# A softmax over 512 columns: stores held back, longer tiles towards the middle, and a first load in two halves

## The chip, the cores and the metric

The kernel runs on one core of a Trainium2 chip. The metric is the device time of one execution in microseconds (us); for the kernel before it is the median of eight runs. A profiled execution also gives a trace: what each engine and each DMA queue did, with times from the span's start.

## What is computed

A softmax along the last axis at temperature 2, on 16 x 1024 rows of 512 float32 numbers:

```python
batch, seq, dim = 16, 1024, 512
x_scaled = x / 2.0
x_max = np.max(x_scaled, axis=-1, keepdims=True)
exp_x = np.exp(x_scaled - x_max)
return exp_x / np.sum(exp_x, axis=-1, keepdims=True)
```

Every input byte is read once and every output byte is written once: 33.55 MB each way.

## The kernel before

The 16,384 rows are spread over the 128 partitions of the on-chip memory, so each partition has 128 rows of 512 floats to do. In what follows a "row" means one such row on every partition, 128 x 512 x 4 = 262,144 bytes. A tile is a group of consecutive rows that is loaded with one DMA and stored with one DMA. `PLAN` (line 11) lists the tiles: for each, how its rows are cut into chunks, and the place at which it stands in an arena of 100 rows (`ARENA`, 204,800 bytes per partition). The first tile has 3 rows, the second 7, then come seven of 15 and others of 7, 3 and 3; the work inside a tile goes by chunks of at most 5 rows.

All 128 rows don't fit in the arena at once. Tiles 0 to 7 (100 rows) have places of their own; tiles 8 to 11 take over the places of earlier ones, and can be loaded only after the stores of those have landed. The dictionary `behind` holds which.

Each chunk goes through three engines, and everything is done in place in the arena:

- VectorE takes the negated maximum of each row (line 85, one instruction for a chunk). It waits for the tile's load.
- ScalarE (ACT) does exp(0.5 x - 0.5 max) and the row sums (line 111, one instruction for a row). It waits for the chunk's maxima, counted by the semaphore `s_max`, and counts its chunks in `s_exp`.
- VectorE takes the reciprocals of the sums (line 94) and multiplies each row by its own (line 98). `s_mul` counts the chunks that are finished.

VectorE's order is written out: the maxima of chunk k, then the multiplies of chunk k - 2 (`LAG`). So while ScalarE works on one chunk, VectorE works on the one ahead and the one behind.

There are two DMA queues. The queue of ScalarE gets the loads of tiles 0 to 7 at the start, two of them ahead of the barrier with which the program begins. The queue of SP (SyncE) gets, in this order, the store of each tile as soon as its last chunk is multiplied (line 134), and, in between, the loads of tiles 8 to 11 (line 139), each after waits for the stores whose place it takes. Loads from the queue of ScalarE and stores from the queue of SP are carried out by the same 16 DMA engines. At the end SP waits for every store (line 141), and the program closes with a barrier of all engines, in which POOL (GpSimd) gathers the others.

Of the kernel before, what the change touches and what calls it, by code (L numbers as in the profile page):

```python
# [1 line left out]

# [4 lines left out]

PLAN = [
    ([3], 0), ([4, 3], 3), ([5] * 3, 10), ([5] * 3, 25), ([5] * 3, 40), ([5] * 3, 55),
    ([5] * 3, 70), ([5] * 3, 85), ([5] * 3, 10), ([4, 3], 3), ([3], 0), ([3], 25),
]
ARENA = 100
LAG = 2


@with_exitstack
def kernel(  # L20
    ctx: ExitStack,
    tc: tile.TileContext,
    x: bass.AP,
    out: bass.AP,
):
    nc = tc.nc
    fp32 = mybir.dt.float32

    xf = x.flatten_outer_dims()
    of = out.flatten_outer_dims()  # L30
    N, D = xf.shape
    P = nc.NUM_PARTITIONS
    n_rows = N // P
    assert sum(sum(c) for c, _ in PLAN) == n_rows

    arena = nc.alloc_sbuf_tensor("arena", (P, ARENA, D), fp32)
    negmax = nc.alloc_sbuf_tensor("negmax", (P, n_rows), fp32)
    sums = nc.alloc_sbuf_tensor("sums", (P, n_rows), fp32)
    recip = nc.alloc_sbuf_tensor("recip", (P, n_rows), fp32)

    tiles, chunks, base = [], [], 0
    for t, (cs, at) in enumerate(PLAN):
        r = sum(cs)
        tiles.append((base, r, at))
        o = 0
        for c in cs:
            chunks.append((t, base + o, c, at + o))
            o += c  # L50
        base += r
    last_chunk = {c[0]: k for k, c in enumerate(chunks)}

    def dram(ap, t):
        b, r, _ = tiles[t]
        return ap[b * P : (b + r) * P].rearrange("(p r) d -> p r d", r=r)

    def sb(t):
        _, r, at = tiles[t]
        return arena[:, at : at + r, :]  # L60


    behind = {}
    for t, (_, r, at) in enumerate(tiles):
        for u in range(t):
            _, ru, au = tiles[u]
            if at < au + ru and au < at + r:
                behind.setdefault(t, []).append(u)

    ld = [tc.alloc_semaphore(f"ld{t}") for t in range(len(tiles))]  # L70
    st = [tc.alloc_semaphore(f"st{t}") for t in range(len(tiles))]
    s_max = tc.alloc_semaphore("s_max")
    s_exp = tc.alloc_semaphore("s_exp")
    s_rec = tc.alloc_semaphore("s_rec")
    s_mul = tc.alloc_semaphore("s_mul")

    def issue_loads(begin, end):

        for t in range(begin, end):
            if t not in behind:  # L80
                nc.scalar.dma_start(out=sb(t), in_=dram(xf, t)).then_inc(ld[t], 16)

    def do_max(k):
        t, b, c, a = chunks[k]
        nc.vector.reduce_max(  # L85
            out=negmax[:, b : b + c],
            in_=arena[:, a : a + c],
            axis=mybir.AxisListType.X,
            negate=True,
        )._wait_ge(ld[t], 16).then_inc(s_max, 1)  # L90

    def do_mul(k):
        t, b, c, a = chunks[k]
        nc.vector.reciprocal(  # L94
            out=recip[:, b : b + c], in_=sums[:, b : b + c]
        )._wait_ge(s_exp, k + 1).then_inc(s_rec, 1)
        for r in range(c):
            ins = nc.vector.tensor_scalar_mul(  # L98
                out=arena[:, a + r],
                in0=arena[:, a + r],  # L100
                scalar1=recip[:, b + r : b + r + 1],
            )
            if r == 0:
                ins._wait_ge(s_rec, k + 1)
        ins.then_inc(s_mul, 1)

    def compute_and_store():

        for k, (t, b, c, a) in enumerate(chunks):
            for r in range(c):  # L110
                ins = nc.scalar.activation(  # L111
                    out=arena[:, a + r],
                    in_=arena[:, a + r],
                    func=mybir.ActivationFunctionType.Exp,
                    bias=negmax[:, b + r : b + r + 1],
                    scale=0.5,
                    accum_out=sums[:, b + r : b + r + 1],
                )
                if r == 0:
                    ins._wait_ge(s_max, k + 1)  # L120
            ins.then_inc(s_exp, 1)


        for k in range(len(chunks) + LAG):
            if k < len(chunks):
                do_max(k)
            if k >= LAG:
                do_mul(k - LAG)


        late = sorted(behind)
        for t in range(len(tiles)):
            nc.sync.wait_ge(s_mul, last_chunk[t] + 1)
            nc.sync.dma_start(out=dram(of, t), in_=sb(t)).then_inc(st[t], 16)
            while late and max(behind[late[0]]) <= t - 2:
                u = late.pop(0)
                for v in behind[u]:
                    nc.sync.wait_ge(st[v], 16)
                nc.sync.dma_start(out=sb(u), in_=dram(xf, u)).then_inc(ld[u], 16)
        for t in range(len(tiles)):  # L140
            nc.sync.wait_ge(st[t], 16)

    hook = nc.inst_callbacks[-1]
    nc.remove_inst_callback(hook)
    symbolic = nc._always_lower_symbolic_ap
    nc._always_lower_symbolic_ap = False
    here = str(nc.cur_bb)
    entry = nc.main_func.blocks[0]  # L150
    head, jumps = entry.instructions[:-5], entry.instructions[-5:]
    entry.instructions = []
    nc.switch_bb("main", None)
    issue_loads(0, 2)
    first = list(entry.instructions)
    at = next(k for k, i in enumerate(head) if type(i).__name__ == "InstDrain")
    entry.instructions = head[:at] + first + head[at:]
    issue_loads(2, len(tiles))
    compute_and_store()
    entry.instructions = list(entry.instructions) + jumps  # L160
    nc.switch_bb(here, None)
    nc._always_lower_symbolic_ap = symbolic
    nc.push_inst_callback(hook)


# [1 line left out]
_INS = ['x']  # L167
_OUTS = [((16, 1024, 512), 'float32')]


# [23 lines left out]
```

## Time and profile before

| What | us |
|---|---|
| Median of eight runs | 162.8 |
| Lowest and highest of the eight | 162.33, 163.19 |
| The profiled execution | 163.17 |
| Its span, first to last instruction | 161.4 |
| VectorE busy | 126.3 |
| ScalarE busy | 94.5 |
| VectorE idle until a load landed | 17.2 |
| ScalarE idle until a chunk's maxima were there | 43.5 |
| First store issued | 14.2 |
| Last store issued | 144.5 |

The sequence of VectorE, with the mean duration of each kind, comes from the groups of instructions with shapes kept apart: a maximum over five rows takes 2814 ns on its own and 2.73 us in sequence, over four 2283 ns, over three 1748 ns; a multiply of one row 482 ns (five in 2.07 us), a reciprocal about 175 ns. An exponential takes 710 ns.

How to read it: the DMA row of the page shows, for 40 equal slices of the span, the mean busy share of the 16 DMA engines in tenths, and the row under it what they moved in GB/s. Busy times of engines are shares of a whole in which any of them, or the DMA engines, may be what the others wait for. Time at the end, after the last instruction of the compute engines, is time in which only DMAs are under way.

### The profile page before, as it was taken

To read this page: it belongs to the slowest core of one execution; us is meant where nothing else is said; L and a number is where in the kernel's file an instruction comes from. 1 tells how busy PE (TensorE), PEld (TensorE's weight loads), DVE (VectorE), ACT (ScalarE), POOL (GpSimd) and SP (SyncE) were. 2 spreads that over 40 slices of the span, in tenths; PEclk is the share of its full clock that TensorE was granted. 3 is DMA by queue.
4 is the path that set the end of the run, shared out by engine and by line. 5 is a ranking of instruction groups with operands and counts; after the bars stand their busy time and mean duration, and the time that the engine had idled before them with its cause. 6 is when DMAs were issued, how large, how long until landed. Compare 5 with 4: busy or idle time off the path is not lost.

```text
span 161.4 us, 513 instructions
## 1 busy us (share of the span) xinstructions
DVE 126.3 (78%) x184; ACT 94.5 (59%) x257; POOL 0.2 (0%) x4
## 2 busy tenths in 40 slices
DVE  0485599999999999998499928999999999970000
ACT  0739087866688666796276651797666875630000
POOL 0000000000000000000000000000000000000000
DMA  7989999899999999999999999999999899999992
GB/s 284 465 388 472 404 439 437 344 447 418 464 381 451 411 457 404 449 434 426 442 411 457 396 459 411 449 402 460 390 434 477 381 472 404 457 434 419 399 418 96
DMA packets 3459, 67.13 MB, mean 416 GB/s; under 512 B 384, under 2 KB 384, under 8 KB 1152
## 3 DMA queue, kind: packets, MB, share of 16 engines
q1 hardware_dynamic: 2304, 40.90, 59.1%
q10 hardware_dynamic: 1152, 26.21, 38.6%
q14 instruction: 3, 0.02, 0.0%
HBM read 33.55 MB, written 33.55 MB: 416 GB/s over the span
## 4 chain that ended last, share of the span: by engine, by line
DVE 74%; DMA 10%; another core or an unknown queue 4%; issue 0%; DVEq 0%
DVE negmax L85 40%; DVE arena L98 32%; DMA arena<-in_x_dram 10%; DVE recip L94 2%; DVEq L189 0%
## 5 line engine op out<-in xcount | busy, mean ns | idle before, releaser
L111 ACT ACTIVATE arena<-arena,negmax 128x512 f32<-128x512 f32 x128 | 90.7, 710 | 43.5 <-DVE negmax L85 43.5
L85 DVE TENSOR_REDUCE negmax<-arena 128x5 f32<-128x2560 f32 (+2 forms) x28 | 72.3, 2586 | 17.2 <-DMA arena<-in_x_dram 17.2
L98 DVE TENSOR_SCALAR arena<-arena,recip 128x512 f32<-128x512 f32 x128 | 53.2, 482 | 1.0
L111 ACT ACTIVATION_READ_ACCUMULATOR arena<-arena,negmax 128x1 f32 x128 | 23.9, 187 | 0.0
L94 DVE RECIPROCAL recip<-sums 128x5 f32<-128x5 f32 (+2 forms) x28 | 4.9, 176 | 0.0
L111 ACT ACT_TABLE_LOAD x1 | 1.3, 1283 | 4.5 <-issue 4.5
L178 POOL MEMSET const-bfloat16-1.0<- 128x1 bf16 x1 | 0.1, 102 | 0.0
L178 POOL MEMSET const-uint8-127<- 128x1 uint8 x1 | 0.1, 102 | 0.0
L178 POOL MEMSET const-float32-0.0<- 128x1 f32 x1 | 0.1, 99 | 0.2 <-issue 0.2
L178 POOL MEMSET const-float32-1.0<- 128x1 f32 x1 | 0.1, 99 | 0.0
## 6 DMA issues: line engine op xcount, KB each, us to landing
out_dram<-arena SPq DMA_DIRECT2D x7, 3840.0 KB, 26.5
arena<-in_x_dram ACTq DMA_DIRECT2D x6, 3840.0 KB, 48.7
arena<-in_x_dram SPq DMA_DIRECT2D x1, 3840.0 KB, 35.9
out_dram<-arena SPq DMA_DIRECT2D x2, 1792.0 KB, 16.2
out_dram<-arena SPq DMA_DIRECT2D x3, 768.0 KB, 15.4
arena<-in_x_dram ACTq DMA_DIRECT2D x1, 1792.0 KB, 8.3
arena<-in_x_dram SPq DMA_DIRECT2D x1, 1792.0 KB, 39.6
arena<-in_x_dram SPq DMA_DIRECT2D x2, 768.0 KB, 38.8
```

What stands on the lines that cost most here:

```text
L85: nc.vector.reduce_max(out=negmax[:, b : b + c], in_=arena[:, a : a + c], axis=mybir.AxisListType.X, negate=True,)._wait_ge(ld[t], 16).the ...
L94: nc.vector.reciprocal(out=recip[:, b : b + c], in_=sums[:, b : b + c])._wait_ge(s_exp, k + 1).then_inc(s_rec, 1)
L98: ins = nc.vector.tensor_scalar_mul(out=arena[:, a + r], in0=arena[:, a + r], scalar1=recip[:, b + r : b + r + 1],)
L111: ins = nc.scalar.activation(out=arena[:, a + r], in_=arena[:, a + r], func=mybir.ActivationFunctionType.Exp, bias=negmax[:, b + r : b + r ...
L178: nc = _bacc.Bacc("TRN2", target_bir_lowering=False, num_devices=1)
```

## The change

The tiles are cut anew: ten instead of twelve, of 3, 5, 9, 15, 21, 21, 21, 15, 11 and 7 rows, and those of 21 rows are worked in chunks of seven. The first seven tiles (95 rows) have places of their own, and tiles 7, 8 and 9 take over places of earlier ones.

- The first tile's load is issued as two DMAs, partitions 0 to 63 from ScalarE's queue and partitions 64 to 127 from SP's (`FIRST`); both stand ahead of the opening barrier, and so does the load of tile 1.
- No store is issued before chunk 4 is multiplied (`HOLD`). The stores of tiles 0, 1 and 2 are issued at that point, one after the other.
- The late loads (tiles 7, 8, 9) move from SP's queue to ScalarE's. Each is issued from ScalarE after the exponentials of the tile that `AFTER` names (tile 4 for tile 7, tile 5 for tiles 8 and 9), after waits on ScalarE for the stores whose place it takes: stores 0, 1 and 2 for tile 7; 2 and 3 for tile 8; 3 for tile 9. SP now has only stores, beside the half of the first load.
- Stores that nobody's load waits for share one semaphore (`s_end`), and the waits at the end are POOL's.

The kernel's arithmetic and VectorE's order, the maxima of chunk k before the multiplies of chunk k - 2, stay.

```diff
--- before.py
+++ after.py
@@ -9,11 +9,19 @@
 
 
 PLAN = [
-    ([3], 0), ([4, 3], 3), ([5] * 3, 10), ([5] * 3, 25), ([5] * 3, 40), ([5] * 3, 55),
-    ([5] * 3, 70), ([5] * 3, 85), ([5] * 3, 10), ([4, 3], 3), ([3], 0), ([3], 25),
+    ([3], 0), ([5], 3), ([5, 4], 8), ([5] * 3, 17), ([7] * 3, 33), ([7] * 3, 54),
+    ([7] * 3, 75), ([5] * 3, 0), ([6, 5], 15), ([4, 3], 26),
 ]
 ARENA = 100
 LAG = 2
+
+HOLD = 4
+
+AFTER = {7: 4, 8: 5, 9: 5}
+
+EARLY = 2
+
+FIRST = [("scalar", [(0, 64)]), ("sync", [(64, 128)])]
 
 
 @with_exitstack
@@ -62,23 +70,34 @@
 
     behind = {}
     for t, (_, r, at) in enumerate(tiles):
+        assert at + r <= ARENA
         for u in range(t):
             _, ru, au = tiles[u]
             if at < au + ru and au < at + r:
                 behind.setdefault(t, []).append(u)
+    awaited = sorted({u for us in behind.values() for u in us})
 
     ld = [tc.alloc_semaphore(f"ld{t}") for t in range(len(tiles))]
-    st = [tc.alloc_semaphore(f"st{t}") for t in range(len(tiles))]
+    st = {t: tc.alloc_semaphore(f"st{t}") for t in awaited}
+    s_end = tc.alloc_semaphore("s_end")
     s_max = tc.alloc_semaphore("s_max")
     s_exp = tc.alloc_semaphore("s_exp")
     s_rec = tc.alloc_semaphore("s_rec")
     s_mul = tc.alloc_semaphore("s_mul")
 
-    def issue_loads(begin, end):
-
-        for t in range(begin, end):
-            if t not in behind:
-                nc.scalar.dma_start(out=sb(t), in_=dram(xf, t)).then_inc(ld[t], 16)
+    def do_load(engine, t, groups=((0, P),)):
+        for u in behind.get(t, []):
+            engine.wait_ge(st[u], 16)
+        for p, q in groups:
+            engine.dma_start(out=sb(t)[p:q], in_=dram(xf, t)[p:q]).then_inc(ld[t], 16)
+
+    def do_early():
+        for name, groups in FIRST:
+            do_load(getattr(nc, name), 0, groups)
+        for t in range(1, EARLY):
+            do_load(nc.scalar, t)
+
+    first_incs = 16 * sum(len(groups) for _, groups in FIRST)
 
     def do_max(k):
         t, b, c, a = chunks[k]
@@ -87,7 +106,7 @@
             in_=arena[:, a : a + c],
             axis=mybir.AxisListType.X,
             negate=True,
-        )._wait_ge(ld[t], 16).then_inc(s_max, 1)
+        )._wait_ge(ld[t], 16 if t else first_incs).then_inc(s_max, 1)
 
     def do_mul(k):
         t, b, c, a = chunks[k]
@@ -104,9 +123,16 @@
                 ins._wait_ge(s_rec, k + 1)
         ins.then_inc(s_mul, 1)
 
-    def compute_and_store():
-
+    def do_rest():
+
+
+        for t in range(EARLY, len(tiles)):
+            if t not in behind:
+                do_load(nc.scalar, t)
+        late = sorted(behind)
         for k, (t, b, c, a) in enumerate(chunks):
+            while late and last_chunk[AFTER[late[0]]] < k:
+                do_load(nc.scalar, late.pop(0))
             for r in range(c):
                 ins = nc.scalar.activation(
                     out=arena[:, a + r],
@@ -128,17 +154,19 @@
                 do_mul(k - LAG)
 
 
-        late = sorted(behind)
+        ends = 0
         for t in range(len(tiles)):
-            nc.sync.wait_ge(s_mul, last_chunk[t] + 1)
-            nc.sync.dma_start(out=dram(of, t), in_=sb(t)).then_inc(st[t], 16)
-            while late and max(behind[late[0]]) <= t - 2:
-                u = late.pop(0)
-                for v in behind[u]:
-                    nc.sync.wait_ge(st[v], 16)
-                nc.sync.dma_start(out=sb(u), in_=dram(xf, u)).then_inc(ld[u], 16)
-        for t in range(len(tiles)):
-            nc.sync.wait_ge(st[t], 16)
+            nc.sync.wait_ge(s_mul, max(last_chunk[t], HOLD) + 1)
+            ins = nc.sync.dma_start(out=dram(of, t), in_=sb(t))
+            if t in awaited:
+                ins.then_inc(st[t], 16)
+            else:
+                ins.then_inc(s_end, 16)
+                ends += 16
+
+        for t in awaited:
+            nc.gpsimd.wait_ge(st[t], 16)
+        nc.gpsimd.wait_ge(s_end, ends)
 
 
 
@@ -151,12 +179,11 @@
     head, jumps = entry.instructions[:-5], entry.instructions[-5:]
     entry.instructions = []
     nc.switch_bb("main", None)
-    issue_loads(0, 2)
+    do_early()
     first = list(entry.instructions)
     at = next(k for k, i in enumerate(head) if type(i).__name__ == "InstDrain")
     entry.instructions = head[:at] + first + head[at:]
-    issue_loads(2, len(tiles))
-    compute_and_store()
+    do_rest()
     entry.instructions = list(entry.instructions) + jumps
     nc.switch_bb(here, None)
     nc._always_lower_symbolic_ap = symbolic
```

## The prediction

> **What bounds the kernel now.** I read the page first: span, busy shares, the DMA rows. 163.17 us is the profiled execution's time, 161.4 its span, so 1.8 us lie outside; the median of the eight runs is 162.8.
>
> ```profile
> span 161.4 us, 513 instructions
> DVE 126.3 (78%) x184; ACT 94.5 (59%) x257; POOL 0.2 (0%) x4
> ...
> DMA  7989999899999999999999999999999899999992
> ...
> DMA packets 3459, 67.13 MB, mean 416 GB/s; under 512 B 384, under 2 KB 384, under 8 KB 1152
> ...
> q1 hardware_dynamic: 2304, 40.90, 59.1%
> q10 hardware_dynamic: 1152, 26.21, 38.6%
> ```
>
> No engine is full, and the DMA row is full from the second slice to the second last. Queue q10 is ACT's (the 100 resident rows of 262,144 B are 26.21 MB), q1 is SP's. Their packets took 59.1 + 38.6 = 97.7% of 161.4 us, so 157.7 us of each DMA engine. The page's chain of waits names VectorE for 74%, but it ends with VectorE's last multiply at 144.5 us. What follows is in the waits of SP's queue and in the DMA view of the last six microseconds:
>
> ```profile
> SPq L141 <- DMA out_dram<-arena: 15.2, 4, 7.4
> ```
>
> ```profile
> DMA  7969978989989999966463440210110100000000
> ...
> DMA packets 257, 1.38 MB, mean 231 GB/s; under 512 B 37, under 2 KB 37, under 8 KB 253
> ...
> q1 hardware_dynamic: 257, 1.38, 55.2%
> ```
>
> SP stands at line 141 for 15.2 us while queued stores drain, until about 160.4. In the last view one digit is 0.15 us (window 155 to 161): from 157.4 the share falls step by step to nothing at about 160. The 16 engines have equal bytes but do not end together: they are busy 0.552 x 6 = 3.3 of the 5 us up to 160, so the last ends about 1.7 us after the average one. Then windows of the whole core (the last column is GB/s, the one before it the DMA share):
>
> ```profile
> 6.00:14.00 8.00, 5.45 (x7) 5.04 (x14) 0.00 (x0) 1.00 1.05 452
> ...
> 18.00:30.00 12.00, 11.89 (x15) 7.79 (x21) 0.00 (x0) 1.00 1.02 430
> 30.00:44.00 14.00, 13.93 (x20) 10.40 (x30) 0.00 (x0) 1.00 1.00 421
> ...
> 60.00:76.00 16.00, 15.89 (x25) 12.13 (x35) 0.00 (x0) 1.00 1.01 434
> ...
> 126.00:148.00 22.00, 18.25 (x36) 11.96 (x34) 0.00 (x0) 1.00 1.00 430
> ```
>
> A packet counts where it starts, so I divide by the share: 430 with loads alone (6 to 14 us), 421 while loads mix with short stores (18 to 44), 430 with an even mix (60 to 76), 430 with SP's queue alone. The kernel is bound by the DMA engines; compute has 15 us to spare at the end. Only three things can shorten it: time before the first byte, lost time per packet or per byte, time after the last byte.
>
> [...] in the DMA view of 20 to 28 us, loads of 30,720-byte and stores of 6,144-byte packets pass nearly one for one:
>
> ```profile
> q10 hardware_dynamic: 86, 2.58, 75.5%
> q1 hardware_dynamic: 98, 0.59, 17.6%
> ```
>
> [...] No run here shows a 64-partition transfer.
>
> **Part by part.** *Fewer, longer packets.* A DMA makes one packet per partition (3459 less 384 semaphore packets and 3 others is 24 DMAs x 128). After: 9 whole loads, two halves, 10 stores = 2560; 512 fewer, 32 per engine. Price of a packet beyond its bytes: the last-six-microseconds view has 220 packets of 6,144 B in 0.552 x 6 x 16 = 53.0 us, 241 ns each. The packet records give 234 ns for one and 1,138 for 30,720 B. 904 ns for 24,576 B is 36.8 ns per KB, so 234 is 226 of bytes and 8 of overhead; with 241 it is 15. Hence 32 x 8 to 15 ns = 0.26 to 0.5 us off; I take 0.35.
>
> *First load in halves.* SP has nothing before its barrier but a drain at 0.0 and ACT issues at 0.13, so SP's half may bring the first byte (1.14 us now) about 0.1 earlier, and the engines start less staggered: 0 to 0.3 gained, I take 0.15. Against it: [...] a 234 ns packet takes up to twice as long; eight packets per engine bound the loss at 8 x 234 = 1.9 us. The engines' first packets start 0.31 us apart, more than one packet[...]; I take 0.2. SP's issue (about 0.4 us) ends before ACT's second issue (until 1.0), which releases the barrier, so nothing waits for it.
>
> *Stores held until chunk 4 is multiplied.* A row costs 262,144 B / 428 GB/s = 0.612 us. Tile 3 (row 32) lands at 1.4 + 32 x 0.612 + about 1.5 (spread and receipt) = 22.5. Then VectorE does max 4, mul 2, max 5, mul 3, max 6, mul 4: 3 x 2.73 + 2 x 2.2 + 1.8 = 14.4, so stores start at 36.9 instead of 14.2. Resident loads (95 rows) last to 1.4 + 58 = 59 without stores, so the engines stay fed; the hold costs nothing by itself. It also makes 18 to 37 us a stretch of loads alone: at 430 instead of 421 that gains 0.4, but 14 to 18 us, still loads alone, ran at 384/0.95 = 404; I take nothing, range -0.6 to +0.6.
>
> *Late loads on ACT with their waits.* Tile 7's load waits for stores 0 to 2 ahead of the exponentials of chunk 10. Store 2 is done when 95 + 17 rows have moved: 1.4 + 112 x 0.612 + 1.5 = 71.4. VectorE from 36.9: max 7, mul 5, max 8, mul 6, max 9 = 3 x 3.8 + 2 x 2.2 gives 52.7; seven exponentials (0.707 each) end at 57.7. So ACT stands 13.7 us, with all later exponentials behind it. VectorE goes on to max 12 (73.1) and then waits for chunk 10's exponentials (71.4 + 0.5 issue + 5.1 = 77.0): 3.9 us idle. Is the DMA fed meanwhile? Store 3 (15 rows, queued since 48.9) lasts to row 127, 79 us; store 4 was queued at 69.3 (mul 9), and with tile 7's 15 rows it lasts to row 163, 101 us; store 5 comes at about 94. Yes, by 7 us.
>
> *The end.* Loads 8 and 9 go out when store 3 lands (about 87) and pass one packet for one beside 43,008-byte store packets (1.59 us): tile 7 until about 94, then 8 x (0.83 + 1.59) = 19 and 8 x (0.54 + 1.59) = 17, so tile 9 lands near 130. VectorE asks for it at about 127 and ends near 142. The DMA's 256 rows end at 1.4 + 157 = 158, the last store needs the final 4.3 us and 1.3 from issue to first byte: compute could be 10 us later at no cost. SP's final waits move to POOL, which gathers the end barrier anyway; the hop from SP to POOL (160.59 to 160.62) goes, 0.05.
>
> Sum: -0.35 - 0.15 + 0.2 - 0.05 = about -0.35 us on 163.17, 162.8; on the median, 162.45, and I round to 162.4 because the tail's stagger (engines end over more than 2 us) can hardly grow.
>
> **Rivals.** *No change, 162.8:* the packet gain is real but the slowest engine decides the end, and its lag comes from slow reads (18 to 60 us), which stay. For: the stagger is several times the gain. Against: every engine has 32 packets less.
>
> *Larger gain, 161.1:* the stretch from 18 to 44 us runs at 430 throughout, 26 us x 2% = 0.5, and the slowest engine's lag of 1.7 shrinks by half, 0.85: 162.45 - 1.35. For: the 421 to 430 step. Against: the 404 at 14 to 18.
>
> *Slower, the halves collide, 164.1:* the 1.9 us above in full, less the 0.55 gained elsewhere = +1.35. Everything after is DMA-bound, so nothing absorbs it. It decides once packets of the first load average over 234 + (550 + 330)/8 = 344 ns, where the loss is 0.33 above that gain. For: same size, same moment on both queues. Against: the stagger.
>
> *Slower, the late loads starve, 166:* should tile 9's landing slip by more than 10 us (one load packet for two store packets would do it) the last store outlives its cover. Against: one for one in the trace.
>
> *The change doing nothing it says* is excluded for the packets[...].
>
> **Chances.** My forecast 0.36, larger gain 0.16, no change 0.27, collision 0.15, starvation 0.06. A difference under about 0.2% (0.33 us) cannot be told from none. Faster 0.52, same 0.27, slower 0.21. The forecast lies just past that bound; its own range is 161.9 to 162.6. For 8 in 10 I reach into both sides: 161.0 to 163.7 takes in the larger gain, no change and half of the collision.
>
> **What will show it.** Right: 2,560 data packets plus 336 semaphore packets, DMA digits of 9 throughout, ACT idle some 14 us near 58 to 71 with no gap in the DMA row, VectorE ending near 142, SP-queue stores draining 15 us after it. Wrong: packets of the first load at 400 ns and more (collision), a DMA digit below 8 between 60 and 110 (starved queue), tile 9 landing past 140, or a tail of well under 2 us (larger gain).

## The result and the profile after

| | us | Ratio to before, 95% interval |
|---|---|---|
| Before, median of 32 runs | 162.79 | |
| After, median of 11 runs | 164.93 | 1.0124 [1.0101, 1.0147] |
| After, the profiled execution and its span | 164.81, 163.0 | |

The changed kernel is slower by 1.24%, about 2 us. The ratio leaves out one slow execution of 166.39 us, which the median counts, so it lies a little below 164.93 / 162.79. The page of after, with the lines that answer to those of before:

```profile
span 163.0 us, 498 instructions
...
DVE  0464989999999999992799999999989607992000
...
DMA  7999899999989997999897999898999999899991
...
DMA packets 2899, 67.13 MB, mean 412 GB/s; under 512 B 336, under 2 KB 336, under 8 KB 592
...
q1 hardware_dynamic: 1520, 33.95, 49.1%
q10 hardware_dynamic: 1376, 33.16, 48.5%
```

The packets are as forecast: 2899 less 336 and 3 is 2560. The queues were busy 97.6% of a longer span, 159.1 us of each DMA engine instead of 157.7, for the same bytes in fewer packets. So the engines were neither idle nor short of work; they took longer over it. The prediction named a DMA digit below 8 between 60 and 110 us as a sign of a starved queue, and the row has two 7s there. They come of the way of counting: the page counts a packet where it starts, and the packets are now up to 1.6 us long in slices of 4.1. With the start and the length of every packet taken from the records, all slices but the first and the last are full.

VectorE's row shows two dents (digits 2 and 0), and the DMA digits beside them are 9. The waits (engine, what it waited for, us in total, times, longest) name the dents:

```profile
DVE negmax L104 <- DMA arena<-in_x_dram: 17.4, 6, 6.5
ACT arena L137 <- DMA out_dram<-arena: 14.2, 1, 14.2
...
DVE recip L113 <- ACT arena L137: 4.0, 1, 4.0
```

ScalarE stands 14.2 us for the stores in front of tile 7's load, and VectorE waits 4.0 us in turn, the first dent: both as worked out (13.7 and 3.9). The second dent is VectorE's wait of 6.5 us for tile 9. That ScalarE's wait costs nothing by itself is seen in e13 below, which has it too (15.0 us) and is faster than before. The time is lost in two other places. The first is the start. Windows of the whole core, 2 to 6 us, before and then after (last columns: DMA share, GB/s):

```profile
2.00:6.00 4.00, 1.41 (x1) 1.28 (x1) 0.00 (x0) 1.00 1.01 413
```

```profile
2.00:6.00 4.00, 0.00 (x0) 1.10 (x1) 0.00 (x0) 1.00 0.99 267
```

The share is full both times, but after moves 267 GB/s instead of 413. Four microseconds at 146 GB/s less are 0.58 MB, 1.4 us at 430 GB/s. A full share with fewer bytes means packets that take longer: by the packet records those of the first load took 455 and 412 ns on average in the two halves of after, 273 in before. The timelines of VectorE show the first maximum, before and after:

```profile
4.59 1.75 DVE L85 TENSOR_REDUCE negmax<-arena 128x3 f32<-128x1536 f32 x1 [4.59 <-DMA arena<-in_x_dram]
```

```profile
6.06 1.75 DVE L104 TENSOR_REDUCE negmax<-arena 128x3 f32<-128x1536 f32 x1 [6.06 <-DMA arena<-in_x_dram]
```

The second is the end, of which after's own profile shows little. The DMA view of after from 155 to 163 us (one digit is 0.2 us):

```profile
DMA  8699598996695995986959101103011000000000
```

In the packet records of before and after, the packets of the last store can be followed engine by engine, end to start. In every chain without a doubtful step, 12 of 16 in before and 7 in after, an engine moves eight of the store's 128 packets and then one of 4 bytes, the semaphore packet (9 ns); before has 384 of these for its 24 DMAs, 16 for each. So the last 16 tell when each engine was done. In after 14 of the 16 are done between 159.4 and 159.9 and two at 161.5 and 161.6; the average is 159.9. In before the average is 158.5 and the last 160.0. So most of the 1.6 us between these two profiled executions, 1.4 us, is a later average, and the last engine's lag behind the average grew only from 1.5 to 1.8 us. (The profiled execution of before, at 163.17, lies above its median of 162.79.)

### The profile page after: what moved, and what is told of

Its sections match the earlier page's. It is cut to its first block, busy times and chain, and to the rows that moved or that the text cites. A ratio compares the mean times of both kernels' runs of the same rounds, so it can differ in the third digit from the quotient of the medians.

```text
span 163.0 us, 498 instructions
## 1 busy us (share of the span) xinstructions
DVE 125.3 (77%) x174; ACT 93.6 (57%) x257; POOL 0.2 (0%) x4
## 2 busy tenths in 40 slices
DMA packets 2899, 67.13 MB, mean 412 GB/s; under 512 B 336, under 2 KB 336, under 8 KB 592
## 4 chain that ended last, share of the span: by engine, by line
DMA 63%; DVE 16%; ACT 9%; ACTq 1%; SPq 0%; issue 0%; DVEq 0%
DMA arena<-in_x_dram 42%; DMA out_dram<-arena 21%; ACT arena L137 9%; DVE arena L117 8%; DVE negmax L104 7%; ACTq L92 1%; SPq L160 0%; DVE recip L113 0%; DVEq L216 0%; ACTq L90 0%
## 5 line engine op out<-in xcount | busy, mean ns | idle before, releaser
L104 DVE TENSOR_REDUCE negmax<-arena 128x5 f32<-128x2560 f32 (+4 forms) x23 | 71.7, 3116 | 17.4 <-DMA arena<-in_x_dram 17.4
L113 DVE RECIPROCAL recip<-sums 128x5 f32<-128x5 f32 (+4 forms) x23 | 4.2, 182 | 4.0 <-ACT arena L137 4.0
```

The source lines that it names most:

```text
L104: nc.vector.reduce_max(out=negmax[:, b : b + c], in_=arena[:, a : a + c], axis=mybir.AxisListType.X, negate=True,)._wait_ge(ld[t], 16 if t ...
L113: nc.vector.reciprocal(out=recip[:, b : b + c], in_=sums[:, b : b + c])._wait_ge(s_exp, k + 1).then_inc(s_rec, 1)
```

## Experiments on the first load

Each ratio is to the kernel before, with its 95% interval. "Collision" stands for the first of the slower rivals of the prediction, packets of the two halves that take up to twice as long; the runs test whether they do, not why. The edits are shown by their main lines; `...` stands for lines that follow from them, mostly the semaphore counts to wait for.

**e1: the first load whole**, all else as changed.

```diff
-FIRST = [("scalar", [(0, 64)]), ("sync", [(64, 128)])]
+FIRST = [("scalar", [(0, 128)])]
```

> The changed kernel with its first load whole, one DMA of 128 partitions on ScalarE's queue; held stores, tiles and late loads as changed. Collision theory ([...] its packets take twice as long): the loss of the first 6 us goes, 1.3 to 2.0 us below the changed kernel, so 162.9 to 163.6 us, ratio to before 1.000 to 1.005, first-load packets back at 234 ns and 2 to 6 us back at over 400 GB/s. Two-queue theory (it is the second queue's issue and its place ahead of the barrier that cost): the same time. Hold theory (the held stores or the late loads on ScalarE cost, the slow reads of 76 to 94 us): stays above 164.3 us, ratio 1.010 or more.

Measured: 163.88 us, 1.0054 [1.0036, 1.0071]. From 1.0124 to 1.0054 is 0.70%, 1.1 us: the halves cost this much, a little under what was expected. 2 to 6 us is back at 419 GB/s, and the median packet of the first load at 234 ns:

```profile
2.00:6.00 4.00, 1.42 (x1) 1.28 (x1) 0.00 (x0) 1.00 1.03 419
```

But 0.54% stays, so the collision is not all of it.

**e2: the kernel before with its first load in halves.**

```diff
-            if t not in behind:
+            if t == 0:
+                nc.scalar.dma_start(out=sb(0)[0:64], in_=dram(xf, 0)[0:64]).then_inc(ld[0], 16)
+                nc.sync.dma_start(out=sb(0)[64:128], in_=dram(xf, 0)[64:128]).then_inc(ld[0], 16)
+            elif t not in behind:
...
```

> The kernel before with only its first load in two halves of the partitions, one on each queue. Collision theory and two-queue theory: 1.3 to 2.0 us slower than before, 164.1 to 164.8 us, ratio 1.008 to 1.012, and 2 to 6 us moves some 270 GB/s instead of 413. Hold theory: no difference beyond 0.3 us.

Measured: 164.19 us, 1.0070 [1.0046, 1.0094], and 230 GB/s from 2 to 6 us:

```profile
2.00:6.00 4.00, 0.00 (x0) 0.58 (x1) 0.00 (x0) 1.00 1.00 230
```

The same 0.7% without any other part of the change, again a little under what was expected.

**e3: two queues still, but split by columns**, so that each DMA reaches all 128 partitions.

```diff
-FIRST = [("scalar", [(0, 64)]), ("sync", [(64, 128)])]
+FIRST = [("scalar", [(0, 768)]), ("sync", [(768, 1536)])]
-            do_load(getattr(nc, name), 0, groups)
+            for p, q in groups:
+                getattr(nc, name).dma_start(out=into[:, p:q], in_=of_x[:, p:q]).then_inc(ld[0], 16)
```

(`into` and `of_x` are tile 0 in the arena and in memory, its three rows as one row of 1536.)

> The changed kernel with the first load still as two DMAs, one on each queue, of the same bytes each, but each over all 128 partitions and half of the row (3,072 bytes a partition). Collision theory: as e1, within 0.3 us, packets near 120 ns. Two-queue theory: as the changed kernel, 164.6 to 165.2 us, ratio above 1.010. Hold theory: above 164.3 us as well.

Measured: 163.47 us, 1.0039 [1.0021, 1.0056]: as e1, within their intervals. By the packet records the 3,072-byte packets take 121 ns at the median. The windows, 2 to 6 us:

```profile
2.00:6.00 4.00, 1.54 (x1) 1.28 (x1) 0.00 (x0) 1.00 1.02 417
```

Two queues at once cost nothing here (1.0039 beside e1's 1.0054); the split by partitions does (1.0124). This decides against the two-queue theory.

**e4: the halves on one queue**, one after the other.

```diff
-FIRST = [("scalar", [(0, 64)]), ("sync", [(64, 128)])]
+FIRST = [("scalar", [(0, 64), (64, 128)])]
```

> The changed kernel with the two halves of the partitions issued one after the other on ScalarE's queue, none on SP's. Collision theory: as slow as the changed kernel or up to 0.4 us slower, 164.6 to 165.3 us, packets of the first load near 450 ns. Two-queue theory: as e1, 162.9 to 163.6 us. Hold theory: above 164.3 us.

Measured: 165.78 us, 1.0158 [1.0114, 1.0203], and 260 GB/s from 2 to 6 us. The loss is there without the second queue, if anything larger than with it and above what was expected; the median packet of the first load took 379 ns instead of 234, where near 450 was expected. (The six executions lie between 164.2 and 166.6 us, so the size is rough.)

**e11: a tile of 15 rows in halves, far from the start.** The kernel before, with tile 2 loaded as two DMAs of 64 partitions on ScalarE's queue.

```diff
+            if t == 2:
+                for p in (0, 64):
+                    nc.scalar.dma_start(out=sb(2)[p : p + 64], in_=dram(xf, 2)[p : p + 64]).then_inc(ld[2], 16)
...
```

> The kernel before with tile 2 (15 rows) loaded as two halves of the partitions, both on ScalarE's queue, about 8 to 27 us, long after the start. The disputed cost enlarged fivefold: 3.9 MB instead of 0.79. Collision theory: packets of this load take up to twice 1,138 ns, so up to 8 x 1.14 = 9.1 us longer, at least 5 [...]: 168 to 172 us, and the loading stretch moves some 220 to 270 GB/s. Start theory (cold queues and first bytes make the loss, not the 64 partitions): within 0.5 us of before.

Measured: 170.89 us, 1.0476 [1.0448, 1.0505], 8.0 us more than the 162.93 beside it, where the bound by doubling was 9.1. The windows of 8 to 26 us, before and then e11:

```profile
8.00:26.00 18.00, 13.25 (x16) 9.92 (x28) 0.00 (x0) 1.00 0.99 418
```

```profile
8.00:26.00 18.00, 5.31 (x6) 5.85 (x18) 0.00 (x0) 1.00 0.96 210
```

The loading stretch runs at half the rate for as long as the halves last: 418 to 210 GB/s at shares of 0.99 and 0.96, a little under the 220 expected at least. So it isn't the cold start. Five times the bytes of the first load cost some five to seven times as much, and nearly all of it arrives at the end: here the DMA engines bound the kernel.

**e15: the halves in the fastest kernel found** (e10 below).

```diff
-FIRST = [("scalar", [(0, 128)])]
+FIRST = [("scalar", [(0, 64)]), ("sync", [(64, 128)])]
```

> e10 (0.9936 of before) with the first load in two halves of the partitions, one on each queue. Collision theory: the halves cost the same 0.7% in a kernel without long tiles: ratio 0.999 to 1.003. If the halves cost only together with the long tiles: at most 0.996.

Measured: 163.33 us, 1.0028 [1.0015, 1.0041] against e10's 0.9936: 0.9%, in a kernel without long tiles, as expected of the collision. The cost of the halves stands by itself.

## Experiments on the other half of the loss

With the first load whole, e1 is 0.54% slower than before, where the sum without the halves' terms (-0.35 - 0.05 us) gives 0.25% faster, so about 0.8% is to be explained. Three runs (e5, e7, e8) undo one part each, and e6 adds one part to the kernel before.

**e5: no hold.** As e1, with

```diff
-HOLD = 4
+HOLD = 0
```

> As e1 (first load whole) but the stores are not held: each is issued when its own last chunk is multiplied. e1 stands at 1.0054 of before although it has 512 packets less; 0.9 us over before is to be explained. Hold theory (long loads alone, then everything at once): 163.2 us or less, ratio at most 1.002. Tile theory (longer packets leave single DMA engines further behind at the end) and queue theory (late loads on ScalarE's queue): within 0.3 us of e1, 163.6 to 164.2 us.

Measured: 162.42 us, 0.9980 [0.9957, 1.0003].

**e6: the kernel before with the hold alone.**

```diff
-            nc.sync.wait_ge(s_mul, last_chunk[t] + 1)
+            nc.sync.wait_ge(s_mul, max(last_chunk[t], 4) + 1)
```

> The kernel before with only the hold: no store before chunk 4 is multiplied. Hold theory: 0.5 to 1.0 us slower than before, ratio 1.003 to 1.006. Tile theory and queue theory: within 0.3 us of before.

Measured: 162.79 us, 1.0000 [0.9986, 1.0014]. The hold costs nothing in the kernel before, with its short tiles and late loads on SP's queue.

**e7: late loads back on SP's queue.** As e1, with the loads of tiles 7 to 9 issued between the stores:

```diff
...
-                do_load(nc.scalar, late.pop(0))
...
+            while late and max(behind[late[0]]) <= t - 2:
+                do_load(nc.sync, late.pop(0))
```

> As e1 but the three late loads go back to SP's queue among the stores, as in the kernel before, so that ScalarE never waits for a store. Queue theory: 163.2 us or less, ratio at most 1.002, and no 14 us idle on ScalarE. Hold theory and tile theory: within 0.3 us of e1.

Measured: 163.00 us, 1.0004 [0.9984, 1.0024].

**e8: the old tiles.** As e1, with the old `PLAN`, and

```diff
-AFTER = {7: 4, 8: 5, 9: 5}
+AFTER = {8: 5, 9: 5, 10: 5, 11: 6}
```

> As e1 but with the tiles of the kernel before (15 rows at most, chunks of 5), the late loads on ScalarE's queue after tiles 5, 5, 5 and 6. Tile theory: 162.6 to 163.2 us, ratio at most 1.002, and the last engine's end within 1.7 us of the average one's. Hold theory and queue theory: 163.7 us or more (0.3 us of it for the packets that come back).

Measured: 162.16 us, 0.9947 [0.9929, 0.9964], faster than before. (It has as many packets as before; what of the hold, the late loads on ScalarE's queue and the waits on POOL gains this 0.5% was not taken apart, and the prediction had only 0.05 us for it.) Each of three parts, taken back alone, returns 0.5% or more, and the hold alone costs nothing: none of my three theories was right as put. The loss belongs to the combination. To be sure of it, e1 and e5 ran again side by side.

**e9 (e1 again) and e12 (e5 again).**

> The kernel of e1 once more, beside e12 on the same chip, since e1 came with other companions than e5 to e8. If the combination of long tiles, hold and late loads on ScalarE really costs: ratio to before 1.003 to 1.007 again. If e1's was a matter of its chip: 0.997 to 1.001.

> The kernel of e5 (first load whole, no hold) once more. If the hold costs with the long tiles: ratio 0.996 to 1.000 and 0.4% or more below e9. If not: equal to e9 within 0.2%.

Measured: e9 163.89 us, 1.0057 [1.0036, 1.0078]; e12 162.85 us, 0.9990 [0.9974, 1.0006]. It is no matter of the chip.

My guess at what the three undone parts share: with the hold, long tiles and a second queue for late loads, loads with short packets stand for long beside stores of 43,008-byte packets, one for one (by after's packet records, 128 packets of 43,008 bytes started while the 128 of tile 8 passed, 98.3 to 116.6 us, and 128 again beside tile 9's, 117.7 to 133.7). The next two runs change packet lengths.

**e13: short store packets.** As e1, the store of a 21-row tile as three DMAs of seven rows.

```diff
-            ins = nc.sync.dma_start(out=dram(of, t), in_=sb(t))
+            step = 7 if tiles[t][1] == 21 else tiles[t][1]
+            for r in range(0, tiles[t][1], step):
+                ins = nc.sync.dma_start(out=dram(of, t)[:, r : r + step], in_=sb(t)[:, r : r + step])
...
```

> As e1 (1.0055 of before), but the store of each 21-row tile goes as three DMAs of seven rows, issued together: packets of 14,336 instead of 43,008 bytes on SP's queue, tiles, hold and loads as in e1. Store-packet theory (a late load passes one packet for one beside 43,008-byte stores, and a slow one of these leaves its DMA engine far behind): ratio 1.000 or less, and tile 9 lands earlier than in e1 because it waits for shorter packets. Load-packet theory and the theory that only the hold itself matters: as e1, 1.004 to 1.007.

Measured: 162.50 us, 0.9977 [0.9967, 0.9987]. This is 0.8% below e1, with 768 packets more. The late loads come sooner beside shorter store packets: by the semaphore packets tile 9 landed at 111.8 us instead of 134.7. VectorE's longest wait for a load is 4.5 us, the one at the start, where e1's was 7.3 for tile 9 (e1, then e13):

```profile
DVE negmax L104 <- DMA arena<-in_x_dram: 16.3, 5, 7.3
```

```profile
DVE negmax L104 <- DMA arena<-in_x_dram: 9.0, 4, 4.5
```

**e14: short load packets.** As e1, the load of a 21-row tile as three DMAs of seven rows.

```diff
-            engine.dma_start(out=sb(t)[p:q], in_=dram(xf, t)[p:q]).then_inc(ld[t], 16)
+        step = 7 if tiles[t][1] == 21 else tiles[t][1]
+        for r in range(0, tiles[t][1], step):
+            engine.dma_start(out=sb(t)[:, r : r + step], in_=dram(xf, t)[:, r : r + step]).then_inc(ld[t], 16)
...
```

> As e1, but the load of each 21-row tile goes as three DMAs of seven rows (14,336-byte packets), stores as in e1. Load-packet theory (43,008-byte reads in a row starve the held stores of tiles 0 to 2, which alternate with them packet for packet): ratio 1.000 or less, and store 0 lands before 48 us instead of 55. Store-packet theory: as e1, 1.004 to 1.007.

Measured: 165.42 us, 1.0179 [1.0139, 1.0218], worse than e1 by 1.2%, which neither theory had. Store 0 landed at 55.0 us (55.7 in e1), not before 48. But the edit did more than shorten packets. ScalarE issues the loads, and with 13 of them at the start it was at it until 20.9 us; its first exponential came at 22.3 us instead of 6.4, and the first store went out at 44.8 instead of 36.7. ScalarE's wait ahead of its work, in e1 and in e14:

```profile
ACT L137 <- issue: 4.0, 1, 4.0
```

```profile
ACT L140 <- issue: 21.0, 1, 21.0
```

So e14 tells nothing clean about load packets: the 1.2% may come of the delay. The load-packet theory is not borne out by it, and e13 stands alone for the store packets. The runs differ in the tail. The DMA views from 155 to 163 us of e1, e13 and e14, in this order (0.2 us a digit):

```profile
DMA  7895995969966133161301100101000000000000
```

```profile
DMA  5999599969996835513000000000000000000000
```

```profile
DMA  9939979969799353161533531505113011000000
```

In all three the share breaks near 157.5 and, by the semaphore packets, nine to eleven of the 16 DMA engines are done by 158.2. The average engine is done at 158.3 in e1, 158.4 in e13 and 159.2 in e14. What differs most is how far the last is behind the average: 0.8 us in e13, 2.8 in e1, 3.0 in e14. e1's profiled execution took 164.29, above its median; e9's, the same kernel at 163.13, shows 1.3. So the lag changes from one execution to the next, and so do the times: the 22 executions of e1 lie within 1.96 us, those of e9 within 1.92, those of e13 within 0.71.

The packet records say more on the lag. All 16 engines are at work from 2 to 157 us, with less than 1.5 us of idle time over the 16 of them together, in before (1.4), after (0.8), e1, e9, e13 and e14. So no late engine had waited for work, and the later issue of e1's last store (147.1 us instead of 139.7 in e13) starved none; if the engines have equal bytes to move, as the eight packets of each in the last stores of before and after suggest, a late one has had slower packets. The stores in SP's queue show such packets. The median of a 43,008-byte one is 1.59 us; of 384, 4 in e1, 9 in e9 and 17 in e14 took over 0.2 us more, up to 0.9. In e13 none of 1,280 packets of 14,336 bytes took more than 0.12 us over the median, and in e8 and e10 none of 896 of 30,720 bytes did (in e14 3 of 256 of that length were slow).

That the length of the store packets is a cause is thus shown by e13 against e1, and slow long packets fit the stagger of the executions profiled. Why a long packet is at times slow isn't shown, nor which engine carried it: the trace doesn't say.

**e10: old tiles, fewer of them.** As e8, the last four tiles (15, 7, 3, 3 rows) as two:

```diff
-    ([5] * 3, 70), ([5] * 3, 85), ([5] * 3, 10), ([4, 3], 3), ([3], 0), ([3], 25),
+    ([5] * 3, 70), ([5] * 3, 85), ([5] * 3, 10), ([5, 5, 3], 25),
-AFTER = {8: 5, 9: 5, 10: 5, 11: 6}
+AFTER = {8: 5, 9: 6}
```

> e8 with its last four tiles (15, 7, 3, 3 rows) cut as two (15 and 13), so ten loads and ten stores, 2,560 packets as in the changed kernel, and no store packet over 30,720 bytes. Packet theory: 512 packets less are worth 0.26 to 0.5 us: 161.7 to 162.0 us, ratio 0.991 to 0.994. If the packets count for nothing: as e8, 162.1 to 162.4 us.

Measured: 162.07 us, 0.9936 [0.9916, 0.9956], the fastest kernel of the study. Against e8's 0.9947 the 512 packets less show as 0.1%, inside the intervals: as expected in sign, but not told from nothing. Its tail, same view as above (the single digit 1 at 161.8 is a packet of the queue q14, kind instruction, not a store):

```profile
DMA  3399633999033300000000000000000000100000
```

A packet counts where it starts, so the digits end one packet early; by the semaphore packets all engines are done by 158.7.

## Why the prediction was wrong

- **Forecast and rivals.** 162.4 us was forecast with 161.0 to 163.7; 164.93 lies outside. The rival of the colliding halves, 164.1 at a chance of 0.15, was right that the packets of the first load take longer (455 and 412 ns on average instead of 273), and had about the right size for its part (+1.1 to +1.5 measured, +1.9 as its bound); it could not cover the second loss.
- **The term for the halves** is the first step that failed. It was mis-sized: 0.2 us taken, with 0.15 gained for an earlier first byte. Measured are 0.7% (e1 against after, e2) to 0.9% (e15), 1.1 to 1.5 us in all. The reason given, that the engines' first packets start 0.31 us apart, failed: by after's packet records the starts spread over 0.37 us and the packets of the two halves still took 455 and 412 ns on average (before: 273, with a median of 234), past the 344 at which this rival was to decide. In e11, away from the start, tile 2's packets took 2.2 us on average instead of 1.15, and the window of 18 us, most of it this load, ran at 210 GB/s instead of 418. That a packet takes up to twice as long was an assumption of the prediction; measured are 1.9 times in e11 and 1.5 to 1.7 times in after's first load. Why packets of 64-partition loads take longer is not shown: the runs give the rate alone.
- **The first byte** came later, not earlier. SP issued at 0.00, but the issue took 0.54 us where 0.4 was assumed, ScalarE's took as long, and the first packet started at 1.31 us instead of 1.14 (packet records). This too goes with the halves and not with two queues: on one queue in e4 the issue of a half took 0.54 us as well, while in e3, with all 128 partitions and two queues, the two issues took 0.37 and 0.38 and the first packet started at 1.00.

```profile
0.00 0.54 SPq L92 DMA_DIRECT2D arena<-in_x_dram  x1
```

- **The packet term** (0.35 us) was right in the number of packets; whether it gains anything stays open (e10 against e8).
- **The hold** at no cost: right in the kernel before (e6), wrong in the changed one, where taking it out gained 0.7% (e5, and e12 against e9). There it is a part of the second loss.
- **ScalarE's wait**, VectorE's 4 us and the fed DMA queues: right, to half a microsecond.
- **The late loads**: tile 9 was to land near 130; in after it landed at 135.3, and VectorE ended at 147.6 instead of 142. The last store still has cover, so the starving rival did not happen. The 19 and 17 us between the landings of tiles 7, 8 and 9 were right (19.4 and 17.1); tile 7 was late, at 98.8 instead of 94. I priced the exchange of short loads with long stores for the landing time alone; the long stores also cost in the tail (e13).
- **The tail** is the second step that failed: "the tail's stagger can hardly grow". The long tiles were given only the gain of fewer packets, and no cost. The end is that of the last DMA engine, and with shorter store packets e1's extra 0.54% is gone (e13). In profiles the last engine's lag is 1.5 us in before (the prediction read 1.7), 1.8 in after, 2.8 and 1.3 in e1 and e9, 0.8 in e13. An estimate for the medians: in before, after, e1, e9 and e13 the profiled execution is 3.2 us longer than the end of its last engine; with the average engine's end of the profiles, the lag at the median is then some 1.1 us in before, 1.9 in after and 2.1 to 2.3 in e1 and e9. So it grew by some 0.8 to 1.2 us; each average end is from one or two profiles.

The 1.24% thus divide into 0.70% for the halves and 0.54% that e1 keeps; that they add up is no test, since e1 divides them. That the first part is 0.7% is borne out by e2, and that shorter store packets remove the second by e13. The range reached to 163.7 by taking in half of the collision; even the collision in full, 164.1, would have been too low.

## What to carry to other kernels

When a kernel is bound by its DMA engines, look at the bytes moved at a full share, not at the share: here DMAs over half of the partitions kept the engines busy (a share of 0.96) and moved half of the bytes (210 GB/s instead of 418, e11). A load that is to go on two queues can be split by columns, at no cost in e3; split by halves of the partitions it cost 0.7 to 0.9%. A packet saved is worth some 8 to 15 ns by the prediction's estimate, which no run here resolved, and longer packets had a price that the estimate left out: in the kernels with stores of 43,008-byte packets the last DMA engine ended 1.3 to 3.0 us behind the average (e1, e9, e14), with 14,336 bytes 0.8 us (e13); and none of the 896 packets of 30,720 bytes in e8 and e10 took more than 0.12 us over the median.

## What the runs showed that had not been expected

- 64-partition loads lost the full factor of two in the steady stretch (210 GB/s instead of 418) and most of it in the cold start, where the windows with their other loads show 267 and 230 with two queues (after, e2) and 260 with one (e4) instead of 413.
- Splitting long stores into three, 768 packets more, made the kernel 0.8% faster; splitting the long loads the same way made it 1.2% slower, with ScalarE held up by issuing them.
- Slow reads (GB/s divided by the share: e1 411 from 60 to 76 us, after 410 from 76 to 94, before 421 from 18 to 44) move about with the plan of the loads, but their sum differs little between the kernels with a whole first load: the packets took 1.4 to 1.9 us per engine more than their medians in before, e1, e3 and e5 to e8. Their sum doesn't explain the differences; how unevenly slow packets fall on the engines may.
